# GLA's first head deals out all of its values between the levels; low-rank gates in two passes; the projection's last token pair finished tile by tile

## The chip, the core and the metric

The kernel runs on one core of a Trainium2 chip. The metric is device time in microseconds (us) of one execution of the whole program. Engines are named as in the profile: PE is TensorE (matmuls), PEld its weight loads, DVE is VectorE, ACT is ScalarE, POOL is GpSimd, SP is SyncE, which only issues DMAs here.

## What is computed

Four layers over 768 tokens (512 latent, 256 context) of width 1024. Layers 0 and 3 mix tokens by gated linear attention (GLA), layer 1 by windowed attention, layer 2 by a gated recurrence (RG-LRU). Around each mixer stand two RMS norms, a modulation by shift and scale, and a gated residual:

```python
for i in range(4):
    shift, scale, gate = jnp.split(silu(c) @ w_mod[i] + b_mod[i], 3, axis=-1)       # and for the context
    h = rmsnorm(x, g_pre[i]) * (1.0 + scale) + shift
    y = mixer_i(h, hc, w_in[i], ..., w_out[i])                                      # context: yc
    x = x + gate * rmsnorm(y, g_post[i])                                            # context: xc, but for the last
# GLA, layers 0 and 3
q, k, v, z = split(h @ w_in)
la[d] = log_sigmoid((h @ w_g1[d]) @ w_g2[d] + b_g[d]) / 16      # d = forward, backward; rank 16
o = gla(q, k, v, la);  o = rmsnorm(o, g_head) * silu(z);  y = o @ w_out
```

## The kernel before

All tensors of tokens stay on the chip; weights are streamed from HBM. A product of two fp32 matrices is made in three matmuls: each operand is split into a high part in the PE's fp32r format and the low rest, and hi*hi, hi*lo and lo*hi are summed in one PSUM bank. `Rh` and `Rl` are the two parts of the layer's input, transposed (8 blocks `k` of 128 channels by 768 tokens). A weight tile is fetched into a buffer `raw` (SP issues the DMA), split by ACT (`wh`, the cast at L266) and DVE or POOL (`wl`, the subtraction at L269); `wh` and `wl` have two buffers each, `raw` two. A new `wh` therefore waits until PE has read the tile two before it.

**Gate weights `g1`.** Both directions' rank-16 matrices are 32 columns wide; `load_g1` copies them into four groups of 32 columns of `wh` (ACT, L286) and their low parts into four groups of `wl` (DVE, L287). Their product `t1` has the gate values four times over, one group on each 32 partitions. It takes 24 matmuls for each piece of tokens (8 blocks, three passes), at L728 in layer 0's start and at L385 in layer 3, where the first pieces are taken early, by `begin` in the `finish` of layer 2. Three of the groups are then multiplied by `g2` (L979; 96 partitions: hi, lo and hi).

**`finish`** (layer i's end). L796 multiplies the mixer's output by `w_out`, whose quarters are `o0` to `o3`: `o0` and `o1` are the two halves of the inner dimension for the first 512 output columns, `o2` and `o3` for the other 512. Token tiles are of 128: 4 and 5 are the context, 0 to 3 the latents. `halves` takes pairs (half, tile) one by one. Then each tile goes through a chain over three engines: `take` (ACT squares with a sum, L803; DVE multiplies by the gate, L804), `post` (DVE sums, L810; POOL mean and `pow`, L614 and L615, give `ry`), `residual` (DVE, L816), `square` (ACT, L621, with L614 and L615 again: `rx`), `scale` (DVE, L823), and by pairs of tiles `norm` in four parts g0 to g3 (PE transposes L638, ACT modulates L642, DVE splits into `Rh` L649 and `Rl` L650). `begin` fills the time: the next layer's first product (L385) for the context and the first latent pair. The modulation vectors of coming layers (`step`: L524, L537, L542) lie between. The order of PE, ACT and DVE in this part is the one that the code is written in (`manual_schedule`); elsewhere a scheduler orders by priority. `convert()` splits the first weight tile of the next layer; its `wh` takes the buffer of `o2`.

**GLA heads.** Each of 4 heads runs through 8 levels of block products (L1062); `spread` deals the head's value product (L1034, 24 matmuls for each of 6 token tiles) and the last head's `z` product out between the levels. `total` says how much is dealt out; what is left runs behind the last level. `outputs` normalises the head's output (L1196 squares, L614 and L615 give `ro`, L1200 scales).

Of the kernel before, what the change touches and what calls it, by code (L numbers as in the profile page):

```python
# [11 lines left out]
F32 = mybir.dt.float32  # L12
F32R = mybir.dt.float32r
# [64 lines left out]
def body(ctx: ExitStack, tc: tile.TileContext, I, out, layers=(0, 1, 2, 3)):  # L78
# [139 lines left out]
    def raw():  # L218
        if raw_pool:
            return raw_pool[0].tile([P, 4, 256], F32, name="rawp", tag="rawp", bufs=10)  # L220
        return wp.tile([P, 4, 256], F32, name="raw", tag="raw")
# [48 lines left out]

    def load_g1(a):

        r = raw()
        rv = r.rearrange("p a b -> p (a b)")[:, 0:256].rearrange("p (k r) -> p k r", k=KC)
        for d in range(2):
            nc.sync.dma_start(
                rv[:, :, d * 16 : (d + 1) * 16],
                I["a_w_g1"][a, d].rearrange("(k p) r -> p k r", p=P),
            )

        def convert():
            w1h = wp.tile([P, KC, 256], F32R, name="wh", tag="wh")
            w1l = wp.tile([P, KC, 256], F32R, name="wl", tag="wl")
            for g in range(4):
                c = slice(32 * g, 32 * g + 32)
                S.copy(w1h[:, :, c], rv)  # L286
                V.tensor_tensor(w1l[:, :, c], rv, w1h[:, :, c].bitcast(F32), op=ALU.subtract)  # L287
            return w1h, w1l

        return convert  # L290

    def load_g2(a, zero=True, load=True):

        r = gpt.rearrange("p j n -> p (j n)")[:, 0:1024].rearrange("p (d n) -> p d n", d=2)
        if a in g2_loaded:
            return r
        if zero:
            (V if a == 0 else G).memset(r, 0.0)
        if load:
            g2_loaded.append(a)  # L300
            for d in range(2):
                for g in range(3):
                    (nc.sync if d else nc.scalar).dma_start(
                        r[32 * g + 16 * d : 32 * g + 16 * d + 16, d, :], I["a_w_g2"][a, d]
                    )
        return r
# [70 lines left out]

    begun = {}

    def ws_part(w, c0, ps, t0, n):  # L380

        R = (Rh, Rl)
        for k in range(KC):
            for u, v in ((0, 0), (0, 1), (1, 0)):
                PE.matmul(  # L385
                    ps, w[u][:, k, c0 : c0 + P], R[v][:, k, t0 : t0 + n],
                    start=(k == 0 and u + v == 0), stop=(k == KC - 1 and u == 1),
                )

    def product_steps(ps, w, c0, t0, n):  # L390
# [217 lines left out]
            run(open_bg.pop())  # L608


    def rstd_of(pool, ss, n, name):
        w = ss.shape[1]
        r = pool.tile([P, w], F32, name=name, tag=name, bufs=4)
        G.tensor_scalar(r, ss, 1.0 / n, EPS, op0=ALU.mult, op1=ALU.add)  # L614
        G.tensor_tensor(r, r, nhalf.to_broadcast([P, w]), op=ALU.pow)  # L615
        return r

    def unit_rstd(pool, x, xn):

        ss = pool.tile([P, 1], F32, name="ssx", tag="ssx", bufs=4)  # L620
        S.activation(xn, x, AF.Square, accum_out=ss)  # L621
        return rstd_of(pool, ss, D, "rx")

    def unit(pool, x, xn):

# [26 lines left out]
    def first_norm(i):  # L652
# [70 lines left out]
        def products(sel, ks):  # L723
            for w, c0, stream, ps in sel:
                t0, n = STREAM[stream]
                for k in ks:
                    for u, v in ((0, 0), (0, 1), (1, 0)):
                        PE.matmul(  # L728
                            ps, w[u][:, k, c0 : c0 + P], (Rh, Rl)[v][:, k, t0 : t0 + n],
                            start=(k == 0 and u + v == 0 and not (w is wqk and stream == "ctx")),  # L730
                            stop=(k == KC - 1 and u == 1), skip_group_check=True,
                        )

        with tc.manual_schedule(engines={PE.engine, S.engine, V.engine}):
# [23 lines left out]
    def finish(i, kc, extra, last, final, xsrc, xdst):  # L758
# [4 lines left out]
        with phase(f"fin{i}", 6, 0) as fp:  # L763
# [36 lines left out]

            def take(ch, tt, ps):
                c = slice(ch * 512, (ch + 1) * 512)
                S.activation(y[tt][:, c], ps, AF.Square, accum_out=ssq[tt][:, ch : ch + 1])  # L803
                V.tensor_tensor(y[tt][:, c], ps, gpt[:, 1 if tt >= 4 else 0, c], op=ALU.mult)  # L804

            rs = {}

            def post(tt):
                s1 = fp.tile([P, 1], F32, name="s1", tag="s1", bufs=4)
                V.tensor_reduce(s1, ssq[tt], axis=AX.X, op=ALU.add)  # L810
                rs[tt] = rstd_of(fp, s1, D, "ry")

            def residual(tt, parts=1):
                for m in range(parts):
# [26 lines left out]
            def halves(*parts):  # L841

                ps = {}
                for kh, tt in parts:
                    if tt not in ps:
                        ps[tt] = mxt()
                    product(w[kh], kh, 1, tt, ps[tt])
                    yield
                    if kh:
                        take(1, tt, ps[tt])  # L850
                        post(tt)
# [26 lines left out]
            def step(pr=None, g=0):  # L878
                second()
                first()  # L880
                if pr:
                    norm(pr, g)

            with tc.manual_schedule(engines={PE.engine, S.engine, V.engine}):
                run(halves((0, 4), (0, 5), (1, 4), (1, 5)))
                h = halves((0, 0), (0, 1), (1, 0), (1, 1))
                residual(4)
                residual(5)
                square(4)
                next(h)  # L890
                square(5)
                scale(4)
                step()
                next(h)
                scale(5)
                if not fill:
                    next(h)
                step((4, 5), 0)
                next(h, None)
                step((4, 5), 1)  # L900
                run(h)
                h = halves((0, 2), (0, 3), (1, 2), (1, 3))
                step((4, 5), 2)
                residual(0)
                next(h)
                step((4, 5), 3)
                residual(1)
                square(0)
                next(h)
                square(1)  # L910
                scale(0)
                step()
                scale(1)
                convert()
                next(h)
                step((0, 1), 0)
                next(h)
                norm((0, 1), 1)
                run(h)
                residual(2)  # L920
                norm((0, 1), 2)
                square(2)
                residual(3)
                norm((0, 1), 3)
                scale(2)
                square(3)
                scale(3)
                begin("ctx")
                begin("lat")
                for g in range(4):  # L930
                    step((2, 3), g)
                while open_f or fill:
                    step()
# [3 lines left out]
    def gla(i, a, ctx_out):  # L937
# [3 lines left out]
        with phase(f"gla{i}") as mp:  # L941

            keep_pool.append(1)
            g2r = load_g2(a)
            w1 = weights("g1")
            t1 = mp.tile([P, T], F32R, name="t1")
            for stream in ("ctx", "lat"):
                t0, n = STREAM[stream]
# [4 lines left out]
                )  # L953

            g2 = mp.tile([P, 2, 512], F32R, name="g2")
            S.copy(g2[:96], g2r[:96])
            G.tensor_tensor(g2[32:64], g2r[32:64], g2[32:64].bitcast(F32), op=ALU.subtract)

            gated = {}
# [1 line left out]
            def gates(h):  # L961
# [11 lines left out]
                for pl in range(2):  # L973
                    d = 1 - pl
                    b = sm[:, 48 + 8 * a + 4 * d + h : 49 + 8 * a + 4 * d + h]
                    ps = sct().rearrange("p c n -> p (c n)")
                    for stream in ("ctx", "lat"):
                        t0, n = STREAM[stream]
                        PE.matmul(  # L979
                            ps[:, t0 : t0 + n], g2[:96, d, h * P : (h + 1) * P], t1[:96, t0 : t0 + n],  # L980
                            start=True, stop=True,
                        )
                    S.activation(tmp[:, pl, :], ps[:, :T], AF.Abs, bias=b)
                    V.tensor_scalar(l1[:, pl, :], ps[:, :T], b, 0.0, op0=ALU.add, op1=ALU.min)
                    yield
# [157 lines left out]
            def outputs(h, X, Y, A, v, tl):  # L1143
# [40 lines left out]
                def chunk(pr):  # L1184
# [8 lines left out]
                        for m, (l, r) in enumerate(tm):  # L1193
                            PE.matmul(ps[:, n, :], l, r, start=(m == 0), stop=(m == len(tm) - 1))  # L1194
                    for n in range(2):
                        S.activation(on[:, n, :], ps[:, n, :], AF.Square, accum_out=ss[:, n : n + 1])  # L1196
                    V.tensor_tensor(on, ps, gh.unsqueeze(1).to_broadcast([P, 2, GDV]), op=ALU.mult)
                    rs = rstd_of(mp, ss, GDV, "ro")
                    for n in range(2):
                        V.tensor_scalar(on[:, n, :], on[:, n, :], rs[:, n : n + 1], None, op0=ALU.mult)  # L1200
                    return on
# [70 lines left out]
            for h in range(GH):  # L1272
# [31 lines left out]

                side = chain(z, values(h, v))
                nz = len(STREAM) * T if ctx_out else len(STREAM) * TL
                nz = nz if prev else 0
                spread(lv, side, len(LEVELS), 24 * (nz + 4 * GDV) / 2.4)
                run(side)
                run(mods(2))  # L1310
                prev = (h, X, Y, A, v, tl)
# [459 lines left out]
```

## Time and profile before

| | us |
|---|---|
| median of 3 runs (lowest, highest) | 1518.22 (1516.42, 1520.79) |
| the profiled execution | 1513.64 |
| its span, first to last instruction | 1511.8 |
| PE busy in the span | 1442.0 (95%) |
| DVE, ACT, POOL busy | 1010.5 (67%), 784.2 (52%), 189.4 (13%) |
| mean granted TensorE clock | 0.990 of full |

The profiled execution is 1.8 us longer than its span; it lies 4.6 us under the median. PE is busy nearly all of the span, so a matmul that goes saves its time wherever PE isn't made to wait for the same length at the next tile; what the other engines do costs only where PE waits.

### The profile page before, as it was taken

What the parts mean: (1) busy time and instruction counts of PE and PEld (TensorE: products, weight loads), DVE (VectorE), ACT (ScalarE), POOL (GpSimd) and SP (SyncE); (2) the same over time, 40 slices, a digit from 0 to 9 for tenths busy, and PEclk for the clock granted to TensorE, in tenths of its full rate; (3) what the DMA queues carried; (4) which work ended last, traced back from release to release, by engine and by line L of the source; (5) the groups of instructions that cost most, each with busy time, mean ns of one, the idle gap of its engine ahead of it and who ended that gap; (6) DMA issues with size and microseconds to landing.
All of it is one profiled execution on the core that took longest, in us unless ns stands there. A gap on an engine that the chain in (4) does not pass through costs nothing.

```text
span 1511.8 us, 29077 instructions
## 1 busy us (share of the span) xinstructions
PE 1442.0 (95%) x11691; PEld 1206.4 (80%) x11691; DVE 1010.5 (67%) x1914; ACT 784.2 (52%) x1541; POOL 189.4 (13%) x300
## 2 busy tenths in 40 slices
PE   5988999999999899999999999899999999999998
PEld 3877888888877778878888787788878778889886
DVE  5576657576264389787883568988972667676854
ACT  5535353624252367656662477878842555364441
POOL 2202100112022200010000210000011211101111
PEclk8999999999999999999999999999999999999999
DMA  9441514112574542122216625212252342121232
GB/s 300 145 147 53 169 38 135 57 34 76 203 237 140 174 112 68 31 65 57 57 56 224 217 79 152 82 50 71 67 177 64 103 145 91 46 60 57 60 111 85
DMA packets 153046, 162.35 MB, mean 107 GB/s; under 512 B 12418, under 2 KB 141968, under 8 KB 152912
## 3 DMA queue, kind: packets, MB, share of 16 engines
q1 hardware_dynamic: 147456, 146.56, 31.4%
q10 hardware_dynamic: 5456, 13.94, 2.6%
q8 instruction: 92, 1.51, 0.4%
q14 instruction: 42, 0.34, 0.1%
HBM read 138.44 MB, written 11.53 MB: 99 GB/s over the span
## 4 chain that ended last, share of the span: by engine, by line
PE 54%; DVE 10%; ACT 5%; DMA 4%; issue 2%; SPq 1%; POOL 1%; ACTq 0%; DVEq 0%; POOLq 0%
PE mxt L796 14%; PE pjt L395 9%; PE pjt L385 9%; PE pjt L1034 4%; PE mxt L1532 3%; PE mxt L1516 2%; PE sct L1637 2%; PE mxt L524 1%; PE mxt L1475 1%; PE mxt L1194 1%; DVE wl L269 1%; PE mxt L1458 1%; DMA bb<-in_b_mod_dram 1%; DMA raw<-in_w_mod_dram 1%; PE sct L1062 1%
## 5 line engine op out<-in xcount | busy, mean ns | idle before, releaser
L385 PE MATMUL pjt<-Rh,wh 128*128 128x256 f32 (+1 forms) x592 | 199.0, 337 | 5.3 <-DVE Rh L649 3.3
L385 PE MATMUL pjt<-Rl,wh 128*128 128x256 f32 (+1 forms) x592 | 198.2, 336 | 2.0 <-DVE Rl L650 1.6
L385 PE MATMUL pjt<-Rh,wl 128*128 128x256 f32 (+1 forms) x592 | 197.1, 334 | 0.7 <-DVE wl L269 0.7
L269 DVE TENSOR_TENSOR wl<-raw,wh 128x1024 fp32r<-128x1024 f32 x106 | 129.7, 1237 | 51.2 <-ACT wh L266 50.6
L395 PE MATMUL pjt<-Rh,wl 128*128 128x512 f32 (+1 forms) x448 | 160.3, 358 | 0.0
L395 PE MATMUL pjt<-Rl,wh 128*128 128x512 f32 (+1 forms) x448 | 159.8, 357 | 0.0
L395 PE MATMUL pjt<-Rh,wh 128*128 128x512 f32 (+1 forms) x448 | 159.5, 356 | 0.0
L266 ACT CAST wh<-raw 128x1024 fp32r<-128x1024 f32 x118 | 121.4, 1051 | 71.6 <-PE mxt L796 33.0
L796 PE MATMUL mxt<-wh,Rh 128*128 128x512 f32 x352 | 138.9, 395 | 0.0
L796 PE MATMUL mxt<-wh,Rl 128*128 128x512 f32 x352 | 137.6, 391 | 0.8 <-DVE Rl L769 0.8
L796 PE MATMUL mxt<-wl,Rh 128*128 128x512 f32 x352 | 137.2, 390 | 0.0
L385 PEld LDWEIGHTS pjt<-Rh,wh 128*128 128x128 f32 x592 | 112.5, 191 | 17.0 <-DVE Rh L649 4.4
L385 PEld LDWEIGHTS pjt<-Rl,wh 128*128 128x128 f32 x592 | 112.6, 190 | 14.6 <-DVE Rl L650 3.8
L385 PEld LDWEIGHTS pjt<-Rh,wl 128*128 128x128 f32 x592 | 112.6, 191 | 12.6 <-DVE wl L269 1.2
L1034 PE MATMUL pjt<-wl,Rh 128*128 128x256 f32 x384 | 110.6, 288 | 0.0
L1034 PE MATMUL pjt<-wh,Rh 128*128 128x256 f32 x384 | 109.8, 286 | 0.0
L1034 PE MATMUL pjt<-wh,Rl 128*128 128x256 f32 x384 | 109.5, 285 | 0.0
L1494 ACT ACTIVATE pe<-mxt,mxs 128x256 f32<-128x256 f32 (+2 forms) x128 | 70.7, 556 | 52.6 <-DVE mxs L1486 51.9
L395 PEld LDWEIGHTS pjt<-Rh,wl 128*128 128x128 f32 x448 | 84.6, 189 | 9.8 <-issue 1.9
L395 PEld LDWEIGHTS pjt<-Rh,wh 128*128 128x128 f32 x448 | 84.7, 189 | 9.2 <-issue 1.2
L395 PEld LDWEIGHTS pjt<-Rl,wh 128*128 128x128 f32 x448 | 84.7, 189 | 9.2 <-issue 1.3
L804 DVE TENSOR_TENSOR y<-mxt,gpt 128x512 f32<-128x512 f32 x44 | 30.3, 689 | 73.9 <-ACT y L803 73.8
(295 smaller groups left out, 3480.9 us busy)
## 6 DMA issues: line engine op xcount, KB each, us to landing
rawp<-in_w_mod_dram SPq DMA_DIRECT2D x48, 512.0 KB, 5.8
raw<-in_w_mod_dram SPq DMA_DIRECT2D x48, 512.0 KB, 4.4
raw<-in_a_w_in_dram SPq DMA_DIRECT2D x32, 512.0 KB, 3.5
raw<-in_b_w_in_dram SPq DMA_DIRECT2D x20, 512.0 KB, 4.9
raw<-in_c_w_in_dram SPq DMA_DIRECT2D x20, 512.0 KB, 3.6
xd<-x SPq DMA_DIRECT2D x18, 512.0 KB
raw<-in_a_w_out_dram SPq DMA_DIRECT2D x16, 512.0 KB, 3.5
x<-xd ACTq DMA_DIRECT2D x16, 512.0 KB, 8.9
```

The lines of the kernel that those rows point to most:

```text
L266: S.copy(h, x)
L269: e.tensor_tensor(l, x, h.bitcast(F32), op=ALU.subtract)
L385: PE.matmul(ps, w[u][:, k, c0 : c0 + P], R[v][:, k, t0 : t0 + n], start=(k == 0 and u + v == 0), stop=(k == KC - 1 and u == 1),)
L395: PE.matmul(ps, w[u][:, k, c0 : c0 + P], R[x][:, k, t0 : t0 + n], start=(k == 0 and u + x == 0), stop=(k == KC - 1 and u == 1),)
L524: PE.matmul(ps[32 * g : 32 * g + 32, 0:256], sT[:, k, :], r2[k // 4][:, k % 4, :], start=(n < 4), stop=(n >= 4), skip_group_check=True,)
L796: PE.matmul(ps, l[:, tt * P : (tt + 1) * P], r, start=(k == 0 and u + v == 0), stop=(k == kc - 1 and u == 1),)
L804: V.tensor_tensor(y[tt][:, c], ps, gpt[:, 1 if tt >= 4 else 0, c], op=ALU.mult)
L1034: PE.matmul(ps[:, n, :], R[u][:, k, tt * P : (tt + 1) * P], w[x][:, k, :], start=(k == 0 and u + x == 0), stop=(k == KC - 1 and u == 1),)
L1494: S.activation(p[:, o : o + w], u[e][:, :w], AF.Exp, bias=nm, scale=0.125, accum_out=den[:, n : n + 1],)
L1516: PE.transpose(u[e][:, c * P : (c + 1) * P], ps[e][:, m * P : (m + 1) * P], ident)
L1532: PE.matmul(po[64 * e : 64 * e + 64, 0:P], v[:, keys[m], 64 * kv : 64 * kv + 64], pt[:, e, m * P : (m + 1) * P], start=(m == len(keys) - 1 ...
L1637: PE.matmul(ps[:, t0 : t0 + nn], wg[a][:, n, :], x[c][:, p0 : p0 + nn], start=(q == 0), stop=(q == 2),)
```

## The change

Four edits. (1) `g1` becomes one tile of four groups, high, high, high, low, and its product two passes (hi and lo of the input): 16 matmuls for a piece instead of 24. `g2` has a fourth group, which is one more DMA for each direction, and L979 reads 128 partitions. (2) The mean of the squares comes out of ACT's square (its scale is 1024^-0.5 or 256^-0.5); POOL's L614 is gone, and `EPS` is added by DVE, in `post` within the sum that was there, for `rx` and `ro` by an instruction of its own. (3) In `finish` the last latent pair's halves are taken as (0,2), (1,2), (0,3), (1,3), tile 2's residual, square and scale come earlier, and tile 3's residual later. (4) Head 0 deals out 6 token tiles of values between the levels instead of 4.

```diff
@@ load_g1, convert
-            w1h = wp.tile([P, KC, 256], F32R, name="wh", tag="wh")
-            w1l = wp.tile([P, KC, 256], F32R, name="wl", tag="wl")
-            for g in range(4):
-                c = slice(32 * g, 32 * g + 32)
-                S.copy(w1h[:, :, c], rv)
-                V.tensor_tensor(w1l[:, :, c], rv, w1h[:, :, c].bitcast(F32), op=ALU.subtract)
-            return w1h, w1l
+            w1 = wp.tile([P, KC, 256], F32R, name="wh", tag="wh")
+            S.copy(w1[:, :, 0:32], rv)
+            V.tensor_tensor(w1[:, :, 96:128], rv, w1[:, :, 0:32].bitcast(F32), op=ALU.subtract)
+            for g in range(1, 3):
+                S.copy(w1[:, :, 32 * g : 32 * g + 32], w1[:, :, 0:32].bitcast(F32))
+            return (w1,)
@@ load_g2
-                for g in range(3):
+                for g in range(4):
@@ ws_part, and the same in layer 0's start
+    def terms(w):
+        return ((0, 0), (0, 1), (1, 0)) if len(w) > 1 else ((0, 0), (0, 1))
-            for u, v in ((0, 0), (0, 1), (1, 0)):
+            for u, v in terms(w):
@@
-    def rstd_of(pool, ss, n, name):
+    def rstd_of(pool, ss, name, eps=True):
         w = ss.shape[1]
         r = pool.tile([P, w], F32, name=name, tag=name, bufs=4)
-        G.tensor_scalar(r, ss, 1.0 / n, EPS, op0=ALU.mult, op1=ALU.add)
-        G.tensor_tensor(r, r, nhalf.to_broadcast([P, w]), op=ALU.pow)
+        if eps:
+            V.tensor_scalar(r, ss, EPS, None, op0=ALU.add)
+        G.tensor_tensor(r, r if eps else ss, nhalf.to_broadcast([P, w]), op=ALU.pow)
@@ unit_rstd (take and outputs alike)
-        S.activation(xn, x, AF.Square, accum_out=ss)
-        return rstd_of(pool, ss, D, "rx")
+        S.activation(xn, x, AF.Square, scale=D ** -0.5, accum_out=ss)
+        return rstd_of(pool, ss, "rx")
@@ post
-                V.tensor_reduce(s1, ssq[tt], axis=AX.X, op=ALU.add)
-                rs[tt] = rstd_of(fp, s1, D, "ry")
+                V.scalar_tensor_tensor(s1, ssq[tt][:, 0:1], EPS, ssq[tt][:, 1:2], op0=ALU.add, op1=ALU.add)
+                rs[tt] = rstd_of(fp, s1, "ry", False)
@@ finish
-                h = halves((0, 2), (0, 3), (1, 2), (1, 3))
+                h = halves((0, 2), (1, 2), (0, 3), (1, 3))
...
                 convert()
                 next(h)
                 step((0, 1), 0)
+                residual(2)
                 next(h)
                 norm((0, 1), 1)
+                square(2)
                 run(h)
-                residual(2)
                 norm((0, 1), 2)
-                square(2)
+                scale(2)
+                norm((0, 1), 3)
                 residual(3)
-                norm((0, 1), 3)
-                scale(2)
                 square(3)
                 scale(3)
@@ gla
-            S.copy(g2[:96], g2r[:96])
+            S.copy(g2, g2r)
-                            ps[:, t0 : t0 + n], g2[:96, d, h * P : (h + 1) * P], t1[:96, t0 : t0 + n],
+                            ps[:, t0 : t0 + n], g2[:, d, h * P : (h + 1) * P], t1[:, t0 : t0 + n],
-                nz = nz if prev else 0
-                spread(lv, side, len(LEVELS), 24 * (nz + 4 * GDV) / 2.4)
+                spread(lv, side, len(LEVELS), 24 * (nz + 4 * GDV if prev else 6 * GDV) / 2.4)
```

Lines from `rstd_of` on are six higher in the changed kernel (L796 is L802, L803 is L809, L816 is L822, L823 is L829), and L266 and L269 are the same.

PE in layer 0's start, the `g1` product's first two blocks, before (`wh`, `wl` are `g1`; 256 is the context, 512 the latents):

```order
L728 MATMUL sct<-Rh,wh 128x256
L728 MATMUL sct<-Rl,wh 128x256
L728 MATMUL sct<-Rh,wl 128x256
L728 MATMUL sct<-Rh,wh 128x256
L728 MATMUL sct<-Rl,wh 128x256
L728 MATMUL sct<-Rh,wl 128x256
```

and now:

```order
L734 MATMUL sct<-Rh,wh 128x256
L734 MATMUL sct<-Rl,wh 128x256
L734 MATMUL sct<-Rh,wh 128x256
L734 MATMUL sct<-Rl,wh 128x256
L734 MATMUL sct<-Rh,wh 128x512
```

Every third matmul, the one with `wl`, is gone; nothing else moves between them.

ACT in layer 0's `finish`, around `convert()`, before (`y0`, `y1` are the latent tiles 0 and 1 and `y2`, `y3` the tiles 2 and 3; `y4` and `y5` here are scratch of `norm`; `wh_4879` is the next layer's first weights):

```order
306 L621 ACTIVATE y1_4328,ssx_4851<-x1_4326 128x1024
307 L537 COPY mp_4876<-mxt_4867 128x256
308 L266 CAST wh_4879<-raw_4530 128x1024
309 L266 CAST wh_4879<-raw_4532 128x1024
310 L537 COPY mp_4916<-mxt_4907 128x256
311 L642 ACTIVATE y4_4316<-mxt_4918,modT_1555 128x256
312 L803 ACTIVATE y2_4332,ssq2_4333<-mxt_4788 128x512
313 L266 CAST wh_5134<-raw_5130 128x1024
314 L642 ACTIVATE y5_4320<-mxt_4946,modT_1555 128x256
315 L803 ACTIVATE y3_4336,ssq3_4337<-mxt_4838 128x512
```

and now (`wh_4855` is the same tile):

```order
308 L627 ACTIVATE y1_4309,ssx_4827<-x1_4307 128x1024
309 L541 COPY mp_4852<-mxt_4843 128x256
310 L266 CAST wh_4855<-raw_4511 128x1024
311 L266 CAST wh_4855<-raw_4513 128x1024
312 L809 ACTIVATE y2_4313,ssq2_4314<-mxt_4765 128x512
313 L541 COPY mp_4899<-mxt_4890 128x256
314 L648 ACTIVATE y4_4297<-mxt_4901,modT_1536 128x256
315 L648 ACTIVATE y5_4301<-mxt_4924,modT_1536 128x256
316 L266 CAST wh_5109<-raw_5105 128x1024
317 L627 ACTIVATE y2_4313,ssx_4933<-x2_4311 128x1024
318 L809 ACTIVATE y3_4317,ssq3_4318<-mxt_4867 128x512
```

Tile 2's `take` moved ahead of `norm` g0, and tile 2's square ahead of tile 3's `take`. The two casts of `convert()` have their old place on ACT; on PE the product (0,3), the last that reads `o2`, stands one product later than before.

DVE in the same `finish`, its tail, before (`x2`, `x3` are tiles 2 and 3; the `Rh`, `Rl` rows are `norm` g2 and g3):

```order
442 L816 SCALAR_TENSOR_TENSOR x2_4330<-y2_4332,ry_4931,x2_4330 128x1024
443 L649 CAST Rh_108<-y4_4316 128x2x256
444 L650 TENSOR_TENSOR Rl_109<-y4_4316,Rh_108 128x2x256
445 L816 SCALAR_TENSOR_TENSOR x3_4334<-y3_4336,ry_4959,x3_4334 128x1024
446 L649 CAST Rh_108<-y5_4320 128x2x256
447 L650 TENSOR_TENSOR Rl_109<-y5_4320,Rh_108 128x2x256
448 L823 TENSOR_SCALAR y2_4332<-x2_4330,rx_4975 128x1024
449 L823 TENSOR_SCALAR y3_4336<-x3_4334,rx_4992 128x1024
```

and now:

```order
465 L655 CAST Rh_108<-y4_4297 128x2x256
466 L656 TENSOR_TENSOR Rl_109<-y4_4297,Rh_108 128x2x256
467 L829 TENSOR_SCALAR y2_4313<-x2_4311,rx_4935 128x1024
468 L655 CAST Rh_108<-y5_4301 128x2x256
469 L656 TENSOR_TENSOR Rl_109<-y5_4301,Rh_108 128x2x256
470 L822 SCALAR_TENSOR_TENSOR x3_4315<-y3_4317,ry_4942,x3_4315 128x1024
471 L620 TENSOR_SCALAR rx_4967<-ssx_4965 128x1
472 L829 TENSOR_SCALAR y3_4317<-x3_4315,rx_4967 128x1024
```

Tile 3's residual went from ahead of g3's split to behind it; tile 2's residual is now further up (row 458), and its scale ahead of g3.

## Rows read from the trace of the kernel before

**Rows 1.** The page: busy time of each engine, share of the span, instructions.

```profile
PE 1442.0 (95%) x11691; PEld 1206.4 (80%) x11691; DVE 1010.5 (67%) x1914; ACT 784.2 (52%) x1541; POOL 189.4 (13%) x300
```

**Rows 2.** Waits of PE, whole span: total us, times, longest.

```profile
PE mxt L524 <- DMA raw<-in_w_mod_dram: 8.3, 9, 1.5
PE sct L1062 <- ACT K L1096: 5.5, 3, 3.4
...
PE mxt L1207 <- DVE on L1200: 1.3, 4, 0.5
```

**Rows 3.** PE's timeline in layer 0: start, us, [idle before].

```profile
41.66 1.07 PE L524 MATMUL pjt<-rawp,sT 128*32 128x256 f32 x16
...
54.13 0.39 PE L728 MATMUL sct<-Rh,wh 128*128 128x512 f32 x1
54.36 0.39 PE L728 MATMUL sct<-Rl,wh 128*128 128x512 f32 x1
...
57.09 0.28 PE L728 MATMUL sct<-Rh,wl 128*128 128x256 f32 x1
57.21 0.28 PE L728 MATMUL sct<-Rh,wh 128*128 128x256 f32 x1
```

**Rows 4.** Stretches: engines' busy us, PEclk (granted clock), DMA share, GB/s.

```profile
34.00:42.00 8.00, 7.72 (x56) 5.46 (x56) 4.04 (x10) 3.97 (x7) 1.78 (x2) 0.86 1.01 289
425.00:475.00 50.00, 46.09 (x363) 35.61 (x361) 31.83 (x64) 25.26 (x52) 11.60 (x17) 1.00 0.60 200
1205.00:1210.00 5.00, 5.00 (x24) 5.00 (x25) 2.90 (x6) 3.74 (x8) 0.00 (x0) 0.50 0.02 3
```

**Rows 5.** ACT's timeline in layer 0's `finish`, the casts of `convert()`.

```profile
440.81 2.00 ACT L266 CAST wh<-raw 128x1024 fp32r<-128x1024 f32 x2
```

**Rows 6.** PE's timeline in layer 0's `finish`: behind the third product, and the tail.

```profile
442.75 0.38 PE L542 MATMUL mxt<-ident,mp 128*128 128x128 f32 x2
...
457.68 0.51 PE L385 MATMUL pjt<-Rh,wh 128*128 128x256 f32 x2 [1.96 <-DVE Rh L649]
...
460.41 0.68 PE L638 MATMUL mxt<-ident,y 128*128 128x128 f32 x4
```

**Rows 7.** DVE's timeline in layer 0's `finish`: residuals 2 and 3, g3's split.

```profile
451.63 1.28 DVE L816 SCALAR_TENSOR_TENSOR x<-y,ry,x 128x1024 f32<-128x1024 f32 x1
...
453.88 3.41 DVE L816 SCALAR_TENSOR_TENSOR x<-y,ry,x 128x1024 f32<-128x1024 f32 x1
457.21 0.41 DVE L649 CAST Rh<-y 128x512 fp32r<-128x512 f32 x1
457.66 0.69 DVE L650 TENSOR_TENSOR Rl<-y,Rh 128x512 fp32r<-128x512 f32 x1
```

**Rows 8.** POOL's timeline beside it.

```profile
453.61 2.59 POOL L269 TENSOR_TENSOR wl<-raw,wh 128x1024 fp32r<-128x1024 f32 x1
```

**Rows 9.** Timeline of layer 1's `finish`: casts, behind the third product, scale 3, transposes.

```profile
861.94 2.01 ACT L266 CAST wh<-raw 128x1024 fp32r<-128x1024 f32 x2
...
863.88 0.38 PE L542 MATMUL mxt<-ident,mp 128*128 128x128 f32 x2
...
878.86 0.75 DVE L823 TENSOR_SCALAR y<-x,rx 128x1024 f32<-128x1024 f32 x1 [0.71 <-POOL rx L615]
...
879.57 0.66 PE L638 MATMUL mxt<-ident,y 128*128 128x128 f32 x4
```

**Rows 10.** Timeline of layer 2's `finish`: `g1` casts, behind the third product, transposes.

```profile
1186.99 1.31 ACT L286 CAST wh<-raw 128x256 fp32r<-128x256 f32 x4
...
1187.89 0.27 PE L638 MATMUL mxt<-ident,y 128*128 128x128 f32 x1
...
1204.83 3.46 PE L638 MATMUL mxt<-ident,y 128*128 128x128 f32 x15 [1.03 <-DVE y L823]
```

**Rows 11.** The groups of POOL's mean: busy us, mean ns.

```profile
L614 POOL TENSOR_SCALAR ro<-sso 128x2 f32<-128x2 f32 x20 | 7.7, 384 | 186.3 <-ACT on L1196 186.0
```

**Rows 12.** POOL's timeline at the program's end, the last tile.

```profile
1506.35 0.19 POOL L614 TENSOR_SCALAR ry<-s 128x1 f32<-128x1 f32 x1 [4.61 <-DVE s L810]
```

More of the change, by code (lines that the diff above doesn't have):

```diff
@@ L383, in ws_part @@
         for k in range(KC):
-            for u, v in ((0, 0), (0, 1), (1, 0)):
+            for u, v in terms(w):
                 PE.matmul(
                     ps, w[u][:, k, c0 : c0 + P], R[v][:, k, t0 : t0 + n],
-                    start=(k == 0 and u + v == 0), stop=(k == KC - 1 and u == 1),
+                    start=(k == 0 and u + v == 0), stop=(k == KC - 1 and (u, v) == terms(w)[-1]),
                 )
@@ L726, in products @@
                 for k in ks:
-                    for u, v in ((0, 0), (0, 1), (1, 0)):
+                    for u, v in terms(w):
                         PE.matmul(
@@ L730, in products @@
                             start=(k == 0 and u + v == 0 and not (w is wqk and stream == "ctx")),
-                            stop=(k == KC - 1 and u == 1), skip_group_check=True,
+                            stop=(k == KC - 1 and (u, v) == terms(w)[-1]), skip_group_check=True,
                         )
@@ L802, in take @@
                 c = slice(ch * 512, (ch + 1) * 512)
-                S.activation(y[tt][:, c], ps, AF.Square, accum_out=ssq[tt][:, ch : ch + 1])
+                S.activation(y[tt][:, c], ps, AF.Square, scale=D ** -0.5, accum_out=ssq[tt][:, ch : ch + 1])
                 V.tensor_tensor(y[tt][:, c], ps, gpt[:, 1 if tt >= 4 else 0, c], op=ALU.mult)
@@ L1195, in chunk @@
                     for n in range(2):
-                        S.activation(on[:, n, :], ps[:, n, :], AF.Square, accum_out=ss[:, n : n + 1])
+                        S.activation(on[:, n, :], ps[:, n, :], AF.Square, scale=GDV ** -0.5, accum_out=ss[:, n : n + 1])
                     V.tensor_tensor(on, ps, gh.unsqueeze(1).to_broadcast([P, 2, GDV]), op=ALU.mult)
-                    rs = rstd_of(mp, ss, GDV, "ro")
+                    rs = rstd_of(mp, ss, "ro")
                     for n in range(2):
```

## The prediction

> **What bounds the kernel now.** I read the busy times first: PE is busy 95% of the span, DVE 67%, ACT 52%, POOL 13% [rows 1]. So a matmul that goes is worth its time, and work on another engine is worth something only where PE waits for it. Second, PE's own waits over the whole span [rows 2]: the largest are for weights (`w_mod`, 8.3 us in nine places) and for one tensor of a GLA head (`K`, 5.5 us in three, 3.4 of it in one); the normalisation of the heads' outputs, which the change shortens, holds PE for 1.3 us in four places. Third, the timelines of the three `finish` parts that the new order rewrites. Layer 0's has one gap on PE that the order explains: 1.96 us for g3's `Rh` [rows 6], which stands on DVE behind tile 3's residual. That residual took 3.41 us against 1.28 for tile 2's [rows 7], and POOL was subtracting weights beside it [rows 8]. In layer 1 PE goes to tile 3's transposes without a wait [rows 9]; in layer 2 it waits 1.03 us for tile 3's scale [rows 10], and afterwards runs at half clock: granted 0.50 over the next 5 us [rows 4].
>
> **The change part by part.** All terms are against the profiled execution, 1513.64 us (span 1511.8 and 1.84 around it).
>
> *Gate weights, layer 0.* A matmul of 256 columns follows the last at 0.12 us, one of 512 at 0.23 [rows 3]. Eight matmuls of each kind go, one for each block: 8 x (0.12 + 0.23) = 2.8 us. Blocks 0 to 3 are multiplied before the modulation product at 41.66 [rows 3], in a stretch in which the DMA engines are busy throughout (share 1.01) and the clock is 0.86 [rows 4]: that product needs the weights that are still being fetched, so I take this half for nothing. The other half, 1.4 us, lies where PE is busy without a break. Term: -1.4 (bounds -2.8 and 0).
>
> *Gate weights, layer 3.* Here 24 matmuls of 256 columns go, 24 x 0.12 = 2.9 us. But 16 of them are the filling of layer 2's `finish`, ahead of tile 3's transposes, where PE waits anyway; taking them out makes that wait longer by the same 1.9 us. Only the last eight, 1.0 us, are behind it. Their effect is in the term of that `finish`. The fewer copies (ACT three for four, DVE one for four) and the additional DMAs of `g2` (ACT and SP four for three) are small beside what these queues wait there; I take zero.
>
> *The new order in `finish`, all three: a wait that the diff does not show.* `convert()`'s casts write into the buffer of `o2`. Before, (0,3) was the second product, long read when ACT came to the casts; now it is the third, and ACT's casts must wait for it. The third product ends at 442.75 in layer 0 [rows 6], while the casts started at 440.81 [rows 5]: 1.94 us later. In layer 1 it is 863.88 - 861.94 = 1.94 [rows 9], in layer 2, whose casts are those of `g1`, 1187.89 - 1186.99 = 0.9 [rows 10]. Queued behind the casts on ACT are tile 2's `take` and the modulation g0; on DVE the two subtractions wait with them, and SP can fetch the next weights only when their `raw` is free.
>
> *Layer 0's tail.* On the chain to tile 3's scale: casts +1.94; tile 3's residual no longer beside POOL's subtraction, 1.28 - 3.41 = -2.13; g3's split (0.41 + 0.69 [rows 7]) and tile 2's scale (0.75 [rows 9]) ahead of that residual, where they stood behind it before and filled the wait for its square, +1.85. If DVE were never idle, that is +1.7; tile 2's `take` now comes early and fills some of its idle time, so I take +1.0. The ends are -0.3 (the casts' delay is absorbed whole) and +3.8 (the residual is still held up). By the order seven more matmuls of the next product, 0.84 us, stand ahead of tile 3's transposes, so PE loses that much less: +0.2 (-1.1 to +3.0).
>
> POOL's subtraction ended at 456.20 (453.61 + 2.59) and the residual 1.09 later, nearly its own 1.28 [rows 7, 8]: it seems to have stood until POOL was done. The Trainium skill, SBUF — State Buffer, section "SBUF: two separate sides", has it so: VectorE with two inputs in SBUF and GpSimd contend for one pair of ports, which is locked for a whole instruction; the trace agrees, and by this rule the hold-up returns whenever POOL starts on the second half of the weights first, which would make the total +1.4 for the -0.7 below.
>
> *Layer 1's tail.* The same +1.94 and +1.85, and no hold-up to win back: +3.8 at the worst, 0 if idle time takes all of it. I take half, about +2, less four more matmuls ahead of the transposes (0.5): +1.5 (-0.5 to +3.3). What is late next is tile 3's scale, for which PE did not wait before.
>
> *Layer 2's tail.* Casts 0.9 late, the same +1.85 at most, so +2.75 at the worst; I take +0.65, since PE's own products there are the shortest and tile 3's `take` waits for PE, not for ACT. Less the 1.0 us of `g1` behind it: -0.3 (-2.9, where all 24 matmuls count, to +1.8).
>
> *rstd.* For the heads' outputs POOL's mean (0.38 us each, 20 of them [rows 11]) is replaced by a DVE addition whose price no row has: it is at least nothing and, being one element on each partition, hardly over POOL's 0.38; but it stands in DVE's queue. PE feels this in four places, 1.3 us in all [rows 2]. Term -0.5 (-1.3 to +1.0). At the end of the program POOL's 0.19 us [rows 12] go from the last tile's chain, which nothing covers, and DVE's sum keeps its place: -0.2. In the `finish` parts the additions are in the tails above.
>
> *Head 0.* The value matmuls are the same in number; only those behind the last level are dealt out ahead. They hide waits between levels or do not. Of the 5.5 us that PE waits for `K`, the longest, 3.4 us, is in layer 0's head 0, before `K` first exists; the order of that head hardly changes. Term 0 (-2.1, the other two waits, to +1.0).
>
> Sum: -1.4 + 0.2 + 1.5 - 0.3 - 0.5 - 0.2 + 0 = -0.7 us: 1512.9 on the profiled execution's scale. That execution is 4.58 us under the median of the runs shown and 2.78 under their lowest; by the median the forecast is 1518.22 - 0.7 = 1517.5 us. About 0.3%, 4.6 us, is what a measurement of this kernel can tell from no change.
>
> **The rivals.**
>
> *The savings land (faster).* The 40 matmuls (2.8 + 2.9 = 5.7 us) count in full, layer 0's 1.96 us gap closes because g3 no longer stands behind a residual, DVE's idle time takes all of the casts' delay, and the small terms hold (0.7): -8.3, 1509.9 us. For it: PE is 95% busy, so removed matmuls usually count, and the gap's cause is taken away by the new order. Against it: 16 of the matmuls stood in front of a wait, and a quarter beside full DMA queues.
>
> *The casts' wait opens a gap on PE before tile 3's transposes, and the clock falls (slower).* With the upper bounds, layer 0's tail is +3.0 and layer 1's +3.3, both idle PE time. Layer 2 shows what follows: after its waits PE ran 5 us at 0.50, level 1.2 of 2.4 GHz, which loses 2.5 us [rows 4]; in layer 1's new gap this would be another 2.5. With the rest (-2.4): +6.4, 1524.6 us. It decides from a gap that lowers the clock; 1.96 us in layer 0 did not (granted 1.00 over that stretch [rows 4, 6]). The Trainium skill, TensorE: Matmul & The Clock Gate, section "What's actually happening", says the same of an idle PE: half of the pulses; the trace agrees with 0.50.
>
> *The weights' transfers give the gain back (no change).* PE waits in nine places for `w_mod` [rows 2]; what layers 0 and 3 gain ahead of such a wait, 1.4 + 1.0, is waited there. The sum is then +1.7, 1519.9 us. Against it: freed buffers let the transfers start earlier too.
>
> **How the numbers follow.** Forecast 0.44, its own range -5 to +4 (1513 to 1522); savings land 0.27; transfers 0.12; clock 0.17. Faster by over 0.3%: nearly all of the savings' case (0.25) and a little of the forecast (0.04), 0.29. Slower: 0.14 of the clock's case, 0.03 of the others, 0.17. The rest is 0.54. The range for 8 in 10 leaves out the outer part of both outer cases: 1509 to 1524 us.
>
> **What would show it.** In the profile after: ACT's casts in layers 0 and 1 waiting for PE's (0,3), released near 442 and 863 less the shift so far; the 1.96 us wait for `Rh` gone, and a wait of PE for tile 3's scale in layers 0 and 1 of one to two us instead; in layer 2 that wait grown from 1.03 towards 3 us; layer 0's product at 41.66 hardly earlier; POOL's L614 absent and L1200 waiting less. The prediction is wrong if layer 1's `finish` isn't longer, if PE doesn't wait for scale 3, or if layer 0's start is shorter by the whole 2.8 us.

## The result and the profile after

The changed kernel takes 1530.83 us (median of five, 1525.41 to 1532.31) against 1518.89 before; the ratio is 1.0076, 95% interval 1.0054 to 1.0098. It is slower by some 11.5 us, 0.8%, outside the forecast range of 1509 to 1524. The profiled execution took 1530.09 us, its span is 1528.3. The kernel before was profiled in a quick execution (1513.64 us; the lowest of the five timed here took 1516.42), so the two traces lie 16.5 us apart, more than the medians. One execution in this document, of `keep_rest_add_first`, took 2617 us and is left out of its ratio.

The page after, which answers to [rows 1]:

```profile
PE 1443.6 (94%) x11651; PEld 1204.7 (79%) x11651; DVE 1015.3 (66%) x1952; ACT 783.3 (51%) x1539; POOL 165.8 (11%) x234
```

40 matmuls are gone, yet PE is not busy for less time (1443.6 for 1442.0). The mean granted clock is lower (0.987 for 0.990), and single executions differ by more than the 5.7 us that these matmuls were worth: `only_spread` below, with as many matmuls as before, has 1447.5. The rest is waiting. PE's waits after (total us, times, longest), which answer to [rows 2]:

```profile
PE mxt L528 <- DMA raw<-in_w_mod_dram: 12.8, 10, 2.9
...
PE mxt L1214 <- DVE on L1207: 6.2, 11, 0.9
PE mxt L644 <- DVE y L829: 4.9, 3, 2.8
PE pjt L389 <- DVE Rl L656: 4.4, 9, 1.8
PE sct L1069 <- ACT K L1103: 4.1, 3, 2.1
```

Four have grown most: `w_mod` 8.3 to 12.8, the heads' outputs 1.3 to 6.2, tile 3's scale 1.8 to 4.9, and `Rl` 1.6 to 4.4. `K` fell from 5.5 to 4.1, `Rh` from 3.3 to 1.4. The shift between the same matmuls of the two traces says where:

| matmul at (us before) | after | shift |
|---|---|---|
| 130.32, layer 0, ahead of the outputs | 128.38 | -1.94 |
| 364.10, behind them | 367.12 | +3.02 |
| 450.06, layer 0's `finish` | 453.08 | +3.02 |
| 466.13, behind its tail | 470.86 | +4.73 |
| 475.20, behind the next `w_mod` product | 481.58 | +6.37 |
| 868.21, layer 1's `finish` | 876.31 | +8.10 |
| 890.09, behind its tail | 900.13 | +10.03 |
| 940.15, behind the next `w_mod` waits | 952.18 | +12.04 |
| 1180.10, layer 2's `finish` | 1191.27 | +11.17 |
| 1240.00, layer 3 | 1251.54 | +11.55 |
| 1460.14, behind its heads | 1477.11 | +16.97 |

The largest steps are the heads of the two GLA layers, +5.0 in layer 0 and +5.4 in layer 3. In layer 0 the wait for the scaled outputs, where I forecast a gain, makes 3.2 us of it (1.3 to 4.5); the waits for `w_mod` make 1.2. In layer 3 the outputs' wait is 1.7 us for none before, and a wait of 1.6 us for `ktl` (L1162) is new, which stands there in all the kernels with the fourth edit and in none without; the other 2 us are not accounted for. One output of layer 0, after (timeline, start and us; other rows left out):

```profile
140.70 0.68 DVE L1204 TENSOR_TENSOR on<-mxt,gh 128x512 f32<-128x512 f32 x1
141.30 0.16 DVE L620 TENSOR_SCALAR ro<-sso 128x2 f32<-128x2 f32 x1
...
141.55 0.69 POOL L621 TENSOR_TENSOR ro<-ro,nhalf 128x2 f32<-128x2 f32 x1 [4.45 <-DVE ro L620]
142.27 0.62 DVE L1207 TENSOR_SCALAR on<-on,ro 128x256 f32<-128x256 f32 x2 [0.81 <-POOL ro L621]
142.77 0.30 PE L1214 MATMUL mxt<-ident,on 128*128 128x128 f32 x1 [0.55 <-DVE on L1207]
```

and the same one before, other rows left out:

```profile
141.44 0.89 POOL L614 TENSOR_SCALAR ro<-sso 128x2 f32<-128x2 f32 x1 [3.81 <-ACT on L1196]
142.19 0.68 DVE L1197 TENSOR_TENSOR on<-mxt,gh 128x512 f32<-128x512 f32 x1
142.41 0.69 POOL L615 TENSOR_TENSOR ro<-ro,nhalf 128x2 f32<-128x2 f32 x1
143.13 0.35 DVE L1200 TENSOR_SCALAR on<-on,ro 128x256 f32<-128x256 f32 x1 [0.26 <-POOL ro L615]
```

Before, POOL's mean followed ACT's square and ran while DVE was still at earlier work; `pow` ran beside DVE's multiplication, and DVE waited 0.26 us. After, the addition takes only 0.16 us, but it stands behind the multiplication in DVE's queue, so `pow` can only start when DVE is done, and DVE then stands idle for all of it, 0.81 us. Over the 20 outputs, DVE's idle time before the scaling (us, times), before and after:

```profile
  POOL ro L615: 3.0, 9
```

```profile
  POOL ro L621: 13.7, 19
```

The second step is tile 3 in the three `finish` parts. PE waits there for `Rl` in layer 0 (2.5 us), for tile 3's scale and `Rl` in layer 1 (1.2 and 1.0), and for the scale in layer 2 (3.6). Layer 0's tail after, DVE's timeline, which answers to [rows 7]:

```profile
457.31 0.42 DVE L655 CAST Rh<-y 128x512 fp32r<-128x512 f32 x1
457.76 2.74 DVE L656 TENSOR_TENSOR Rl<-y,Rh 128x512 fp32r<-128x512 f32 x1
460.42 1.27 DVE L822 SCALAR_TENSOR_TENSOR x<-y,ry,x 128x1024 f32<-128x1024 f32 x1
462.91 0.15 DVE L620 TENSOR_SCALAR rx<-ssx 128x1 f32<-128x1 f32 x1 [1.21 <-ACT y L627]
463.79 0.75 DVE L829 TENSOR_SCALAR y<-x,rx 128x1024 f32<-128x1024 f32 x1 [0.73 <-POOL rx L621]
```

POOL's beside it, which answers to [rows 8]:

```profile
457.46 2.49 POOL L269 TENSOR_TENSOR wl<-raw,wh 128x1024 fp32r<-128x1024 f32 x1 [1.06 <-ACT wh L266]
```

The hold-up beside POOL has not gone, it has moved: before, the residual took 3.41 us; now g3's `Rl`, usually 0.69, takes 2.74, beside POOL's subtraction (457.46 to 459.95), and PE waits for that `Rl` (1.80 us). Then the residual comes last, and its chain over ACT and POOL is bare: DVE is idle for 1.21 and 0.73 us. The casts did wait as forecast (ACT L266 at 446.02, after 2.09 us idle, for which the view names no releaser; PE's third product ran until 445.9).

In all, though, PE waits no longer in this tail than before (2.6 us in both traces). What layer 0's tail loses, +1.7, goes with the clock: it is granted at 0.50 behind the wait for `Rl`, for 3.3 us in which PE is busy throughout, and half of that is some 1.7 us of work; before, it was 1.00 there [rows 4]. After (columns as in [rows 4]):

```profile
461.50:464.80 3.30, 3.30 (x24) 1.90 (x23) 1.32 (x5) 1.52 (x3) 0.55 (x1) 0.50 0.78 290
```

### The profile page after: what moved, and what is told of

Same layout as the page of the kernel before. It is cut to its first block, busy times and chain, and to the rows that moved or that the text cites. A ratio compares the mean times of both kernels' runs of the same rounds, so it can differ in the third digit from the quotient of the medians.

```text
span 1528.3 us, 28949 instructions
## 1 busy us (share of the span) xinstructions
PE 1443.6 (94%) x11651; PEld 1204.7 (79%) x11651; DVE 1015.3 (66%) x1952; ACT 783.3 (51%) x1539; POOL 165.8 (11%) x234
## 4 chain that ended last, share of the span: by engine, by line
PE 46%; DVE 12%; ACT 8%; DMA 5%; issue 3%; POOL 1%; SPq 1%; DVEq 0%; ACTq 0%; POOLq 0%
PE mxt L802 14%; PE pjt L399 8%; PE pjt L389 7%; PE pjt L1041 4%; PE mxt L1538 3%; PE mxt L1522 2%; DMA raw<-in_w_mod_dram 2%; PE sct L1643 2%; PE mxt L528 1%; DMA bb<-in_b_mod_dram 1%; DVE wl L269 1%; PE mxt L1481 1%; PE mxt L1464 1%; ACT wh L266 1%; DVE Rl L656 1%
## 5 line engine op out<-in xcount | busy, mean ns | idle before, releaser
L389 PE MATMUL pjt<-Rh,wl 128*128 128x256 f32 (+1 forms) x568 | 190.3, 336 | 0.7 <-DVE wl L269 0.7
L269 DVE TENSOR_TENSOR wl<-raw,wh 128x1024 fp32r<-128x1024 f32 x106 | 129.8, 1238 | 51.3 <-ACT wh L266 50.8
L266 ACT CAST wh<-raw 128x1024 fp32r<-128x1024 f32 x118 | 121.3, 1050 | 73.1 <-PE mxt L802 33.5
L802 PE MATMUL mxt<-wh,Rh 128*128 128x512 f32 x352 | 139.0, 395 | 0.0
L802 PE MATMUL mxt<-wh,Rl 128*128 128x512 f32 x352 | 137.7, 391 | 0.8 <-DVE Rl L775 0.8
L802 PE MATMUL mxt<-wl,Rh 128*128 128x512 f32 x352 | 137.4, 390 | 0.0
L389 PEld LDWEIGHTS pjt<-Rh,wl 128*128 128x128 f32 x568 | 108.0, 190 | 12.7 <-DVE wl L269 1.2
L399 PEld LDWEIGHTS pjt<-Rh,wl 128*128 128x128 f32 x448 | 85.0, 190 | 9.9 <-issue 1.9
L810 DVE TENSOR_TENSOR y<-mxt,gpt 128x512 f32<-128x512 f32 x44 | 30.4, 690 | 75.6 <-ACT y L809 75.4
```

Source lines behind the costliest of these rows:

```text
L266: S.copy(h, x)
L269: e.tensor_tensor(l, x, h.bitcast(F32), op=ALU.subtract)
L389: PE.matmul(ps, w[u][:, k, c0 : c0 + P], R[v][:, k, t0 : t0 + n], start=(k == 0 and u + v == 0), stop=(k == KC - 1 and (u, v) == terms(w)[ ...
L399: PE.matmul(ps, w[u][:, k, c0 : c0 + P], R[x][:, k, t0 : t0 + n], start=(k == 0 and u + x == 0), stop=(k == KC - 1 and u == 1),)
L802: PE.matmul(ps, l[:, tt * P : (tt + 1) * P], r, start=(k == 0 and u + v == 0), stop=(k == kc - 1 and u == 1),)
```

## The experiments

All ratios are against the kernel before, from runs on the same chip; 0.001 is 1.5 us.

### The four edits one by one

`only_g1`, `only_rstd`, `only_order` and `only_spread` are the kernel before with one edit of the change each.

> The kernel before with the first edit alone (gate weights in two passes, g2 in four groups). Queue theory (the loss sits in the head outputs' added instruction on DVE and in the new finish order): this part is harmless and gains, -2 to -4 us against before (layer 0's second half 1.4, layer 3 one to two). Rival (the additional g2 DMAs and the later release of weight buffers shift the w_mod transfers, so the loss sits here): +2 us or more.

1516.18 us, 0.9995 (0.9986 to 1.0005): -0.8 us, at most 2.1 gained.

> The kernel before with the second edit alone (mean inside ACT's square, EPS added by DVE). Queue theory: DVE's addition stands behind its multiplication in each of the 20 head outputs, so POOL's pow no longer runs beside the multiplication; PE waits for the scaled output in about ten places instead of four, 6 us instead of 1.3: +6 to +10 us. Rival (the new finish order carries the whole loss, POOL's saved instruction is worth something): -1 to +1 us.

1522.39 us, 1.0031 (1.0020 to 1.0042): +4.7 us. PE's wait, and what DVE waited for ahead of the scaling (L1202 here):

```profile
PE mxt L1209 <- DVE on L1202: 6.1, 10, 0.9
```

```profile
  POOL ro L617: 13.8, 19
```

These are the changed kernel's numbers (6.2 and 13.7) with this edit alone; in the other three kernels the wait is 1.3 us in four places, as before. The queue theory holds, its size a little under what I expected.

> The kernel before with the third edit alone (the last latent pair tile by tile). Casts theory: the next layer's casts wait for the third product, raw buffers come free later, and behind each of layers 0 and 1 the w_mod transfer is late by 1.5 us as well: +4 to +7 us. Rival (the loss is all in the head outputs, the order gains or loses nothing): -2 to +1 us.

1521.86 us, 1.0032 (1.0020 to 1.0044): +4.9 us, the size as expected; whether by the casts is asked below. The shifts in its trace: +1.9 over layer 0's tail, +2.0 over layer 1's, +1.9 over layer 2's; the `w_mod` waits (8.9 us) are hardly longer than before (8.3, and 8.7 in the copy below), so the second half of the casts theory, late transfers, fails.

> The kernel before with the fourth edit alone (head 0 deals out six tiles of values). The shift between the two traces falls by about 1.3 us where layer 0's head 0 waits for K (3.4 us before, 2.1 after). If this edit does that: -1 to -2 us. If the shorter wait came from another edit: 0 within 0.5 us.

1517.98 us, 1.0007 (0.9994 to 1.0021): nothing that the time shows. `K` is waited for 5.5 us as before; it is in `only_g1` that this wait is 4.1. The trace has a small cost: in layer 3's heads PE now waits 1.2 us for `ktl`, and the shift grows there by 1.2 us, where it stays within 0.2 in every trace with neither this edit nor the second.

The four sum to +9.8 us, the change measured +11.5: within their intervals the parts add up.

### The place of the addition

```diff
# ro_on_pool, on the changed kernel
-                    rs = rstd_of(mp, ss, "ro")
+                    rs = mp.tile([P, 2], F32, name="ro", tag="ro", bufs=4)
+                    G.tensor_scalar(rs, ss, EPS, None, op0=ALU.add)
+                    G.tensor_tensor(rs, rs, nhalf.to_broadcast([P, 2]), op=ALU.pow)
# ro_add_first, on the changed kernel
+                    rs = rstd_of(mp, ss, "ro")
                     V.tensor_tensor(on, ps, gh.unsqueeze(1).to_broadcast([P, 2, GDV]), op=ALU.mult)
-                    rs = rstd_of(mp, ss, "ro")
```

> The changed kernel, only that the head outputs' EPS is added on POOL again, straight from the mean that ACT's square gives, as before. Queue theory: pow runs beside DVE's multiplication again, PE's wait for the scaled output falls from 6.2 us in eleven places to about 1.3 in four: 4 to 6 us faster than the changed kernel, so +5 to +8 us against before (what is left is the order of the finish parts). Rival (the wait comes from elsewhere, for example from what ACT queues ahead of the squares): as slow as the changed kernel, +10 to +13 us.

1520.51 us, 1.0013 (0.9997 to 1.0029): some 9 us faster than the changed kernel, more than expected.

> The changed kernel with DVE's addition issued ahead of its multiplication in each head output, nothing else. Queue theory: it is the place in DVE's queue that costs, not the engine: pow runs beside the multiplication, the wait falls to 1 to 2 us, +5 to +8 us against before, as with the addition on POOL. Rival (the hop over a third engine costs, wherever it stands in the queue): the wait stays near 6 us, +10 to +13 us.

1522.05 us, 1.0032 (1.0019 to 1.0045): 6 to 7 us faster. PE's wait for the scaled output, first with POOL's addition, then with DVE's ahead of the multiplication:

```profile
PE mxt L1216 <- DVE on L1209: 1.6, 5, 0.5
```

```profile
  PE mxt L1214: 0.7, 2
```

For this wait, then, DVE's instruction isn't the price: ahead of the multiplication it is no worse than POOL's, 0.7 us against 1.3 before. Its place in the queue is.

It is not free everywhere, though. Over layer 3's heads (1240.00 to 1460.14 before) the shift grows by 5.4 us in the changed kernel, by 1.6 with POOL's addition, but still by 4.1 with DVE's addition ahead of the multiplication (2.9 and 3.4 in the two versions for use below). Of each, 1.2 us go with the fourth edit (`only_spread`); what the rest is stays open.

### What delays tile 3

```diff
# order_casts_late, on only_order
-                convert()
                 next(h)
+                convert()
                 step((0, 1), 0)
# order_res3_early, on only_order
                 norm((0, 1), 2)
-                scale(2)
-                norm((0, 1), 3)
                 residual(3)
+                norm((0, 1), 3)
+                scale(2)
                 square(3)
```

> The kernel before with the new order of finish, but the two casts for the next layer issued behind tile 2's take on ACT instead of ahead of it. Casts theory, in its first form (tile 2's chain is held up behind the casts that wait for the third product): tile 2's take starts some 2 us earlier, tile 3's scale with it, 2 to 4 us faster than the new order alone, so +1 to +3 us against before. Rival (the casts' wait was on the way of the weights, not of tile 2; or the loss is g3's split and tile 2's scale standing ahead of tile 3's residual): +4 to +6 us, as the order alone.

1520.41 us, 1.0021 (1.0007 to 1.0035): between the two, not told apart by the time. In the trace tile 2's `take` starts at 442.74 instead of 448.82 with the order alone; that trace is 2.0 us earlier at this place anyway, so some 4 us are the casts' doing. Still layer 0's tail shifts by +2.1 as with the order alone. But PE is idle for 2.6 us in that tail in both traces as in the one before, and in both the clock is granted at 0.50 for some 3 us, so this shift tells nothing of the casts. In layer 1, where the clock stays at 1.00, they may be part of it (+1.3 for +2.0).

> The kernel before with the new order of finish, but tile 3's residual back ahead of norm g3 (and tile 2's scale behind g3), as it was. Bare chain theory: behind its residual tile 3 still needs ACT's square and POOL's two steps, 2.1 us in which DVE has nothing left since g3's split and tile 2's scale were drawn ahead of it; with those behind the residual again the chain is covered, and the loss of the order, 2 us in each of three finishes, goes: -1 to +2 us against before (the order alone: +4.9). Rival (the casts' wait for the third product is what delays tile 3): +3 to +6 us.

1517.84 us, 1.000 (0.999 to 1.001): the order's loss is gone, to within 1.5 us. DVE's idle time before `scale` (us, times, longest), first the order alone, then this:

```profile
DVE y L823 <- POOL rx L615: 13.9, 15, 2.1
```

```profile
DVE y L823 <- POOL rx L615: 7.5, 12, 0.7
```

The longest, 2.13 us, stood in all three tails, behind tile 3's residual. With g3's split and tile 2's scale behind the residual again, they fill that time, and PE's wait for tile 3's scale falls from 5.4 to 1.2 us. The rest of the new order, with the casts that wait for the third product still in it, costs and gains nothing that the time shows. Where the 5 us come back the trace shows only in part: PE waits 3.6 us for `Rh` again (3.3 before, none with the order alone), and layer 1's tail still shifts by +1.5.

The clock is a second cause in layer 0's tail, with the order or without it. It falls to 0.50 there for some 3 us in six of the seven traces with the new order (shifts of +1.0 to +2.1); in the seventh, `ro_add_first`, it stays at 1.00, and the tail shifts by +0.8. But it also falls in `g2_dma_only` and `g1_three_g2` below, which have the old order (+1.4 and +1.3); in the other traces with the old order it does not, and their shifts are within 0.2. What makes it fall there isn't shown: PE had waited 1.80 us just before it in the changed kernel, and 1.96 us at the same place before, where it did not fall.

### What becomes of the gate weights' matmuls

In every kernel with two passes PE waits 10.6 to 13.3 us for `w_mod`'s raw tiles, in every one without 6.3 to 9.7.

```diff
# g2_dma_only, on the kernel before; g1_three_g2, on only_g1, the reverse
-                for g in range(3):
+                for g in range(4):
```

> The kernel before, with the fourth group of g2 fetched (one more small DMA for each direction in both GLA layers, four in all) and not used. Open: the gate weights' part takes 40 matmuls (5.7 us) away and gains 0.8; in each trace with this part PE waits 10.6 to 13.3 us for w_mod's raw tiles, in each without it 6.3 to 9.7. Theory A (the additional DMAs do it: every later transfer moves on by one in the order of the queues): the wait before layer 1's first w_mod product rises from 1.3 to 2.7 us or more and the total over 10, and the time by 2 to 4 us. Theory B (the earlier PE waits for transfers that do not come earlier): waits as before, 8 to 9.7 us, the time within 1 us.

1518.57 us, 1.0011 (0.9996 to 1.0026); the wait is 9.2 us.

> The kernel before with the gate weights in two passes, but the fourth group of g2 left zero: the product of the gate weights' low part is left out, and no DMA is added. Theory A (the additional DMAs move the later transfers): waits for w_mod back at 6 to 9.7 us, 3 to 5 us faster than before. Theory B (PE comes earlier to transfers that do not): the waits stay at 10.6 us or more, as with this part alone, -0.8 us against before.

1514.59 us, 0.9986 (0.9969 to 1.0003); the wait is 12.3 us. So it is the two passes, not the DMAs, after which PE waits longer for these weights, as theory B had it, though this kernel's time, -2.1 (-4.7 to +0.5), lies between the two expectations and does not decide. The largest such wait, ahead of layer 1's first `w_mod` product, is 2.84 us here and 1.25 before. Why it grows even there, a whole layer after the removed matmuls, stays open.

### Versions for use, and the noise

> A version for use: the gate weights in two passes, six tiles of values in head 0 and the new rstd with DVE's addition ahead of its multiplication in the head outputs, with the old order of finish. Queue theory: the parts without their two losses, -1 to -3 us against before. Rival (the additions cost in the finish parts and the start as well, since DVE's queue is fuller there): +1 to +4 us.

1517.01 us, 0.9996 (0.9983 to 1.0008): no different from before.

> The changed kernel with both losses mended: DVE's addition ahead of its multiplication in the head outputs, and tile 3's residual ahead of g3. If the two causes are the whole loss: -2 to +1 us against before, 10 us faster than the changed kernel. If something else of the change costs (g2's additional DMAs, the additions in the finish parts): +3 to +6 us.

1521.38 us, 1.0018 (1.0003 to 1.0034), from 1514.29 to 1527.60: 9 us faster than the changed kernel, but still 2.7 us (0.5 to 5.2) behind the kernel before, where I expected -2 to +1. So the two causes are most of the loss and perhaps not all of it. Its profiled execution is its fastest and spanned 1512.5 us, near before's best; what its slower executions lose isn't settled.

> The kernel before, unchanged, profiled once more and timed against itself: how far two traces of one program lie apart, and whether a ratio of 0.3% means anything. Expected: 0 within 1 us; in the trace the waits for the head outputs 1.3 us in four places again, those for weights (w_mod) and the start's DMAs different by up to 3 us.

1517.10 us, 1.000 (0.9987 to 1.0012). In its trace the same matmuls shift by up to 2.2 us against the first trace (at 240 and at 364), the outputs' wait is 1.3 us in four places, and `w_mod`'s 8.7. Part of that shift is the clock: from 120.7 to 124.0 us it is granted at 0.50 in the copy, and it was 1.00 there in the first trace. Shifts of 2 us in one place are therefore no evidence by themselves; the groups of waits are better.

No version beats the kernel before by more than can be measured.

## Why the prediction was wrong

- *rstd, forecast -0.5 (bounds -1.3 to +1.0): +4.7.* This is the step that failed. I saw that the addition "stands in DVE's queue" and priced only its duration, which was no error (0.16 us). I left out what stands ahead of it, the 0.68 us multiplication with which POOL's `pow` had run in parallel, and so that 0.69 us of `pow` became bare in nearly all of 20 outputs. My bound of +1.0 was too narrow: 20 outputs by some 0.7 us would have given up to 14 us, DVE's idle time grew by 10.7, and PE felt 4.9 of it.
- *The order of `finish`.* Terms +0.2, +1.5 and about +0.65 for layer 2 without `g1`, +2.35 in all; measured +4.9, so this sum was mis-sized. Layer 1 was near (+2.0 in the trace of the order alone); layer 2 was too low (+1.9). The wait of the casts is there as forecast, but it was the wrong reason: what decided by the time was the +1.85 for g3's split and tile 2's scale ahead of the residual, which I took to be absorbed in part. In layer 0 the -2.13 for the residual did not come, since the hold-up went to g3's `Rl`, as the sentence on the Trainium skill had allowed; but PE's waits there came out as long as before, and the +1.9 of the trace goes with a fall of the clock that I had ruled out for this tail.
- *The gate weights.* Forecast -2.4, measured -0.8 (-2.1 to +0.8). Layer 0's -1.4 is not shown: the shift at 66.02 is -1.48 in `only_g1`, but +1.17 in the changed kernel, and +1.47 in `only_order`, where nothing ahead of it was changed. Layer 3's -1.0 did come: from layer 2's `finish` (1180.10) to layer 3 (1240.00) the shift of `only_g1` falls by 1.3. The waits for `w_mod` grew by 2.9 in that trace: the rival in which the transfers give the gain back was right for this part.
- *Head 0, forecast 0:* +1.0 (-0.9 to +3.2), nothing that the time shows; the 1.2 us of layer 3's `ktl` I had not thought of.
- *The clock.* The slower rival had a gap lower it in layer 1. There it stayed at 1.00 (889 to 894 us in the changed kernel) in spite of a wait of 1.2 us. It fell in layer 0's tail instead, and in layer 2's it is at 0.50 for 10.2 us where it was for 6.8. Since kernels that lose nothing show the first fall too, it is a part of single traces rather than the cause of the 11.5 us.

## What to carry to other kernels

An instruction added to an in-order queue costs what its place makes wait, not what it takes: here 0.16 us stood behind 0.68 us of work that had run in parallel with the next engine's step. Before moving a step of a chain over several engines, look at what stands ahead of it and behind it on its engine: the last tile's chain needs other work after it to cover its hops. Before giving a shift between two traces to a wait, read the granted clock of that stretch in both. And a hold-up of two engines on each other moves with the work that meets there; taking one instruction out of it puts the next one in.

## What was unexpected of the hardware

A DVE subtraction of 128x512 took 2.74 us instead of 0.69 beside POOL's 128x1024 subtraction, and ended 0.55 us after it; in the kernel with the residual early it was a cast (L649) from 0.42 to 2.57. In layer 0's tail it is each time the first DVE instruction to start behind POOL's: in the changed kernel the cast that started at 457.31, ahead of POOL's 457.46, took its usual 0.42. A DVE multiplication that reads PSUM (L810, at 393.08) took its usual 0.69 wholly beside another of these subtractions (392.55 to 394.95). And it can go the other way: at 375.45 POOL's subtraction takes 5.48 us beside seven DVE instructions of their usual lengths.
